# TensorE's instructions in the order in which the source writes them, in a hybrid attention layer

## The chip, the core and the metric

The kernel runs on one core of one Trainium2 chip. The metric is device time in microseconds (us) of one execution of the whole layer; lower is better.

## The reference

One decoder layer over 2048 positions of width 1024, in float32. A normalised input is projected by one matrix into queries, keys, values and gates of two mixers. Mixer A attends over a window of 128 positions with a learned sink per head; mixer B attends under three dilated patterns and merges them by their softmax denominators. Both results are gated, joined, projected out and added to the input.

```python
hdn = rmsnorm(x, norm_gain[i])
proj = jnp.einsum("bsd,de->bse", hdn, w_in[i])
q_a, k_a, v_a, g_a, q_b, k_b, v_b, g_b = jnp.split(proj, split_at, axis=-1)
...
o_a, _, _ = banded_attention(q_a, k_a, v_a, A_WINDOW - 1, sinks=sinks_a[i])
o_a = o_a.reshape(b, S, A_WIDTH).astype(x.dtype) * jax.nn.silu(g_a)
...
o_b = dilated_attention(q_b, k_b, v_b)
o_b = o_b.reshape(b, S, B_WIDTH).astype(x.dtype) * jax.nn.silu(g_b)

mixed = jnp.concatenate([o_a, o_b], axis=-1)
x = x + jnp.einsum("bse,ed->bsd", mixed, w_out[i])
```

## The kernel before

**Stages.** The work is cut into eight stages (line 26): four of mixer B with two heads each, two of mixer A with four query heads each, and two halves of the output projection. A stage goes over four blocks of 512 positions, a block over two halves of 256. Each half multiplies its inputs by the stage's weights: for every 128 positions (`tt`) 24 matmuls into a PSUM tile `pj` (line 244), then the gates, 24 matmuls for each 128 gate columns into another `pj`. Every product is made of three matmuls, since operands are split into a high and a low part (`wh`, `wl`, `xh`, `xl`) for precision.

**Behind a projection** stand three chains. `norm_rope`, `norm_factors` and `norm_split` (lines 406 to 461) normalise and rotate queries and keys on VectorE, ScalarE and GpSimd; `finish` and `qk_transposes` (lines 342 and 463) then transpose them on TensorE and copy the result out of PSUM. For the first stage, `rstd` (line 193) sums squares of x with four small matmuls, takes the root on GpSimd, and `rb_make` (line 208) transposes the result on TensorE.

**Attention units.** One head of one block is a unit of four steps: `scores` (matmuls into `sc`, then a masked maximum on VectorE, lines 598 and 813, and an exponential on ScalarE, lines 599 and 814), `transposes` (TensorE turns the probabilities `P` into `pt`; `split_p`, lines 573 and 574, copies them out as a high part on ScalarE and a low part on VectorE), `pv` (matmuls with the values into `po`), and `after`. A unit over the window (lines 590 to 645, and 719 to 735 in mixer A) works in four blocks of 128 queries. A dilated unit (lines 808 to 849) makes a triangle of scores in three `sc` tiles, whose first holds two of the four query blocks, and three `pt` tiles.

**Buffers.** PSUM holds two tiles of each of the names `pj`, `sc`, `pt` and `po`: a third tile of a name begins when the first has been read out.

**The order.** The source itself interleaves: `proj` is a generator that yields after every few matmuls, and `advance` (line 931) then issues one step of a unit, so that the steps keep pace with the projection by their estimated costs. The program is then handed to the scheduler of the tile framework, which takes the source's order as priorities and issues on each engine what its timing simulation finds ready. So a step that waits lets later instructions of the same engine pass. All DMAs are issued by SyncE (SP).

The steps of the prediction touch these lines: 198 (`rstd`), 211 (`rb_make`), 244 (projection), 475, 485, 490, 491 and 499 (`qk_transposes`), 590 and 591 (window scores), 619, 625 and 719 (their transposes), 645 and 735 (their products), 808 and 809 (dilated scores), 828 and 835 (their transposes), 849 (their product).

Of the kernel before, what the change touches and what calls it, by code (L numbers as in the profile page):

```python
# [32 lines left out]
@with_exitstack  # L33
def hybrid_layer(ctx, tc, xT, xn, x, wB, wA, wO, ng, gains, sinks, rot, masks, ident, out):
    nc = tc.nc
    PS = bass.MemoryType.PSUM
    const = ctx.enter_context(tc.tile_pool(name="const", bufs=1))
    wp = ctx.enter_context(tc.tile_pool(name="wp", bufs=1))
# [2 lines left out]
    wk = ctx.enter_context(tc.tile_pool(name="wk", bufs=2))  # L41
    ps = ctx.enter_context(tc.tile_pool(name="ps", bufs=1, space=PS))

# [996 lines left out]
```

## Time and profile before

| | us |
|---|---|
| median of 3 runs | 1261.07 (1257.18 to 1261.21) |
| profiled execution, its own time | 1261.51 |
| profiled execution, span of its instructions | 1259.4 |

The page is one execution on the chip. Busy time of an engine is the union of its instructions. Matmuls overlap: one lasts longer from its start to its end than the time until the next may start, so TensorE (PE) counts as busy through short waits. PEld are its weight loads, which run ahead of the matmuls. DVE is VectorE, ACT ScalarE, POOL GpSimd. "L244" is line 244 of the kernel. A row of waits names who waited, for whose result, how long in total, how often, and the longest. PEclk is the share of its full clock that TensorE was granted.

### The profile page before, as it was taken

The page shows a single profiled execution, that of the slowest core. Times are in us where ns is not written, and L with a number is a line of the kernel's source. Part 1 is how long each engine was busy: PE and PEld are TensorE (multiplying, and loading weights), DVE is VectorE, ACT ScalarE, POOL GpSimd, SP SyncE. Part 2 cuts the span into 40 slices and gives each one's busy share as a digit, 9 for nine tenths or more (in the row PEclk, how much of TensorE's full clock was granted, in tenths as well). Part 3 has the DMA queues.
Part 4 walks back from the last instruction along what each step waited for, and adds up shares of the span by engine and source line. Part 5 has one row for each costly group of instructions (what it writes and reads, how often), then busy time and mean ns, then how long its engine had stood idle before and what let it go on. Part 6 is the DMA issues. An engine that isn't in the chain of part 4 may idle for free.

```text
span 1259.4 us, 25438 instructions
## 1 busy us (share of the span) xinstructions
PE 1174.8 (93%) x8328; PEld 1141.3 (91%) x8328; DVE 850.7 (68%) x2288; ACT 834.7 (66%) x2418; POOL 680.4 (54%) x788
## 2 busy tenths in 40 slices
PE   6898979899899798899998999999999999999899
PEld 5898979899799798888997999898899998999898
DVE  5676768678677678776777788789868877522221
ACT  6477868678677687676777677677776776522221
POOL 4886734566645574536576567565655554333122
PEclk9899989999899899899998999999999999999999
DMA  7454677877687667687775764545333225566561
GB/s 215 120 166 127 193 226 212 229 200 212 182 250 207 210 190 201 189 244 204 199 210 172 228 203 143 150 137 167 114 97 94 80 89 165 163 192 211 166 191 69
DMA packets 196883, 220.98 MB, mean 175 GB/s; under 512 B 34312, under 2 KB 143632, under 8 KB 196752
## 3 DMA queue, kind: packets, MB, share of 16 engines
q1 hardware_dynamic: 196752, 219.37, 59.3%
q8 instruction: 66, 1.08, 0.4%
q14 instruction: 65, 0.53, 0.1%
HBM read 164.44 MB, written 54.86 MB: 174 GB/s over the span
## 4 chain that ended last, share of the span: by engine, by line
PE 55%; DMA 16%; DVE 10%; ACT 8%; POOL 6%; issue 3%; SPq 2%; POOLq 0%; ACTq 0%; DVEq 0%
PE pj L244 39%; DMA xs<-in_xT 3%; DMA Rb<-rD 2%; DMA stg<-in_wB 2%; PE po L849 2%; DMA stg<-in_wO 2%; DMA stg<-in_wA 2%; PE sc L590 1%; PE sc L591 1%; PE po L645 1%; PE pt L828 1%; PE po L735 1%; PE pt L719 1%; ACT P L599 1%; DVE ptl L574 1%
## 5 line engine op out<-in xcount | busy, mean ns | idle before, releaser
L244 PE MATMUL pj<-wh,xh 128*128 128x384 f32 (+1 forms) x1008 | 332.8, 332 | 12.2 <-ACT wh L104 5.5
L244 PE MATMUL pj<-wl,xh 128*128 128x384 f32 (+1 forms) x1008 | 334.4, 332 | 0.8 <-DVE wl L102 0.7
L244 PE MATMUL pj<-wh,xl 128*128 128x384 f32 (+1 forms) x1008 | 333.4, 331 | 1.3 <-DVE xl L157 1.3
L157 POOL TENSOR_TENSOR xl<-xs,xh 128x512 fp32r<-128x512 f32 x158 | 210.3, 1341 | 146.3 <-ACT xh L155 136.6
L155 ACT ACTIVATE xh<-xs 128x512 fp32r<-128x512 f32 x252 | 154.5, 629 | 123.6 <-PE pj L244 100.6
L244 PEld LDWEIGHTS pj<-wh,xh 128*128 128x128 f32 x1008 | 194.0, 193 | 15.7 <-ACT wh L104 5.8
L244 PEld LDWEIGHTS pj<-wl,xh 128*128 128x128 f32 x1008 | 194.8, 193 | 3.2 <-DVE wl L102 1.1
L244 PEld LDWEIGHTS pj<-wh,xl 128*128 128x128 f32 x1008 | 194.4, 193 | 3.0 <-DVE xl L157 1.6
L574 DVE TENSOR_TENSOR ptl<-pt,pth 128x512 fp32r<-128x512 f32 (+3 forms) x232 | 142.0, 619 | 35.5 <-ACT pth L573 31.8
L244 PE MATMUL pj<-xh,wgh 128*128 128x256 f32 x496 | 147.7, 298 | 17.9 <-DVE V L311 12.0
L244 PE MATMUL pj<-xh,wgl 128*128 128x256 f32 x496 | 145.8, 294 | 0.0
L244 PE MATMUL pj<-xl,wgh 128*128 128x256 f32 x496 | 145.4, 293 | 0.0
L573 ACT ACTIVATE pth<-pt 128x512 fp32r<-128x512 f32 (+3 forms) x232 | 123.1, 543 | 23.1 <-PE pt L719 8.1
L431 POOL TENSOR_TENSOR t<-t,t 128x256 f32<-128x256 f32 (+1 forms) x96 | 78.1, 814 | 77.9 <-DVE t L422 57.2
L244 PEld LDWEIGHTS pj<-xh,wgh 128*128 128x128 f32 x496 | 97.8, 197 | 19.7 <-ACT klz L502 5.9
L244 PEld LDWEIGHTS pj<-xl,wgh 128*128 128x128 f32 x496 | 97.8, 197 | 0.6
L244 PEld LDWEIGHTS pj<-xh,wgl 128*128 128x128 f32 x496 | 97.4, 196 | 0.9 <-DVE wgl L105 0.2
L814 ACT ACTIVATE P<-P,scD 128x256 f32<-128x256 f32 (+3 forms) x128 | 71.6, 560 | 33.6 <-DVE scD L813 32.9
L157 DVE TENSOR_TENSOR xl<-xs,xh 128x512 fp32r<-128x512 f32 x94 | 76.9, 823 | 21.1 <-ACT xh L155 20.5
L447 DVE TENSOR_TENSOR t<-t,fac 128x256 f32<-128x256 f32 (+1 forms) x96 | 67.4, 710 | 30.8 <-POOL fac L182 23.7
L182 POOL TENSOR_TENSOR fac<-un,mhalf 128x8 f32<-128x8 f32 (+1 forms) x48 | 85.4, 1779 | 2.5
L813 DVE CUSTOM_DVE_ANT_0 P<-sc,mk 128x256 f32<-128x256 f32 (+3 forms) x128 | 61.1, 484 | 32.2 <-PE sc L809 31.5
(188 smaller groups left out, 3082.8 us busy)
## 6 DMA issues: line engine op xcount, KB each, us to landing
xs<-in_xT SPq DMA_DIRECT2D x94, 512.0 KB
xs<-mx SPq DMA_DIRECT2D x32, 512.0 KB
vd<-V SPq DMA_DIRECT2D x64, 128.0 KB
qd<-qc SPq DMA_DIRECT2D x32, 256.0 KB
TT<-tab SPq DMA_DIRECT2D x32, 256.0 KB
cv<-vd SPq DMA_DIRECT2D x32, 256.0 KB
cq<-qd SPq DMA_DIRECT2D x32, 256.0 KB
ck<-kd SPq DMA_DIRECT2D x64, 128.0 KB
```

What stands on the lines that cost most here:

```text
L155: nc.scalar.activation(h, f, AF.Copy)
L157: eng.tensor_tensor(l, f, f32(h), op=OP.subtract)
L182: nc.gpsimd.tensor_tensor(y, u, mhalf.to_broadcast([128, n]), op=OP.pow)
L244: nc.tensor.matmul(o, a, b, start=first and n == 0, stop=last and n == 2, skip_group_check=True)
L431: nc.gpsimd.tensor_tensor(t1[:, :n], t1[:, :n], t2[:, :n], op=OP.add)
L447: nc.vector.tensor_tensor(t1v, t1v, fac[:, tt, :, None].to_broadcast([128, nh, 64]), op=OP.mult)
L573: nc.scalar.activation(hi, pt, AF.Copy)
L574: nc.vector.tensor_tensor(lo, pt, f32(hi), op=OP.subtract)
L590: nc.tensor.matmul(sc[:, j, :], q[h // 2][:, h % 2, i, :], kw, start=True, stop=False)
L813: nc.vector.tensor_tensor_reduce(pd, o[:, :m], m2[:, 512 - m:], -0.125, BIG, OP.add, OP.min, nb)
L814: nc.scalar.activation(pd, pd, AF.Exp, bias=nb, scale=-1.0, accum_out=l)
L849: nc.tensor.matmul(po[:, o:o + w], a, b, start=n_ == 0, stop=n_ == len(seq) - 1, skip_group_check=True)
```

## The change

One line is added at the head of `hybrid_layer`:

```diff
     nc = tc.nc
+    ctx.enter_context(tc.manual_schedule(engines={mybir.EngineType.PE}))
     PS = bass.MemoryType.PSUM
```

Inside this context TensorE's instructions stay in the order in which the source issues them. The scheduler still orders the other four engines and SyncE's DMAs, now around that fixed order. The instructions are the same: 8296 matmul instructions before and after, and the same number of operations on every other engine. All source lines move down by one, so line 828 before is line 829 after, and the numbers in tile names grow by two.

**Dilated unit.** TensorE, fourth stage, last block, the unit whose probabilities are `P_10230` before and `P_10232` after; `pt` tiles are its three transposed tiles, `pj` is the projection beside it, `po` the product of another unit. Before:

```order
L828 MATMUL pt_10360<-idf_75,P_10230 128x128
L244 MATMUL pj_10334<-wh_9499,xh_10284 128x384
L828 MATMUL pt_10360<-idf_75,P_10230 128x128 x2
L244 MATMUL pj_10334<-wl_9500,xh_10284 128x384
L849 MATMUL po_10338<-ptl_88,cv_9884 128x256 x2
L828 MATMUL pt_10367<-idf_75,P_10230 128x128 x2
L244 MATMUL pj_10334<-wh_9499,xl_10285 128x384
```

After, the same unit:

```order
L245 MATMUL pj_10336<-wh_9488,xl_10151 128x384
L829 MATMUL pt_10362<-idf_77,P_10232 128x128 x4
L829 MATMUL pt_10369<-idf_77,P_10232 128x128 x3
L836 MATMUL pt_10375<-idf_77,P_10232 128x128 x3
L245 MATMUL pj_10336<-wh_9501,xh_10286 128x384
```

Before, the transposes are strewn among the projection's matmuls, and the third tile (line 835) comes 28 rows after the last transpose into the second; after, all ten stand in one piece.

**Window unit of mixer A.** TensorE, the unit with probabilities `P_14224` before and `P_14226` after; `sc` tiles take its scores, `pt_14188` and `po_14250` belong to other units. Before:

```order
L719 MATMUL pt_14188<-idf_75,P_13894 128x128 x4
L590 MATMUL sc_14225<-KK_13431,Q_13429 128x256
L591 MATMUL sc_14225<-klz1_90,Q_13429 128x256
L590 MATMUL sc_14225<-KK_13431,Q_13429 128x256
L591 MATMUL sc_14225<-klz1_90,Q_13429 128x256
L244 MATMUL pj_14176<-xh_13835,wgh_12729 128x256
```

After:

```order
L591 MATMUL sc_14227<-KK_13433,Q_13431 128x256
L592 MATMUL sc_14227<-klz1_92,Q_13431 128x256
L591 MATMUL sc_14227<-KK_13433,Q_13431 128x256
L592 MATMUL sc_14227<-klz1_92,Q_13431 128x256
L591 MATMUL sc_14236<-KK_13433,Q_13431 128x256
L592 MATMUL sc_14236<-klz1_92,Q_13431 128x256
L591 MATMUL sc_14236<-KK_13433,Q_13431 128x256
L592 MATMUL sc_14236<-klz1_92,Q_13431 128x256
L672 MATMUL po_14250<-idf_77,eA_14245 8x128
L720 MATMUL pt_14256<-idf_77,P_14226 128x128 x4
L720 MATMUL pt_14263<-idf_77,P_14226 128x128 x4
```

Before, 37 more rows stand between these four score matmuls and the unit's first transposes, and the last two of its eight score matmuls come only behind those; after, one row stands between all eight and the transposes.

**The start.** TensorE, first half; `po` holds the transposed root of `rb_make`, `sc` the projection of the second half. Before:

```order
L244 MATMUL pt_404<-xh_171,wgl_249 128x256
L211 MATMUL po_305<-idf_75,rst_83 128x128 x2
L198 MATMUL po_381<-one_81,o1c_321 128x1 x4
L244 MATMUL sc_462<-wh_135,xl_365 128x384
L244 MATMUL sc_462<-wh_144,xh_364 128x384
```

After:

```order
L199 MATMUL po_207<-one_83,o1c_195 128x1 x4
L245 MATMUL pj_263<-wh_117,xh_112 128x384
L245 MATMUL pj_263<-wl_118,xh_112 128x384
L245 MATMUL pj_263<-wh_117,xl_113 128x384
L245 MATMUL pj_263<-wh_126,xh_112 128x384
```

These five rows open TensorE's program after: the sums of squares come ahead of the first projection, and `rb_make` (line 212) follows right behind that projection's 24 matmuls. Before, 97 rows of matmuls stand ahead of `rb_make`. SP and POOL begin with the same operations in the same order in both programs, through GpSimd's first root (line 182).

## The prediction

> **What bounds the kernel now.** I read the page's engine rows first, then the waits of TensorE, then its timeline at the steps that the change moves.
>
> ```profile
> span 1259.4 us, 25438 instructions
> PE 1174.8 (93%) x8328; PEld 1141.3 (91%) x8328; DVE 850.7 (68%) x2288; ACT 834.7 (66%) x2418; POOL 680.4 (54%) x788
> ```
>
> TensorE is the bound: 1174.8 of 1259.4 us, next VectorE with 68%. So 84.6 us of it are idle, and no order of the same instructions can win more than these and what a low clock costs. The waits show who ends the idle time:
>
> ```profile
> PE pj L244 <- DVE V L311: 13.2, 7, 5.7
> PE sc L591 <- ACT klz L502: 5.8, 2, 4.7
> PE pj L244 <- ACT wh L104: 5.5, 1, 5.5
> PE pt L828 <- DVE ptl L574: 5.2, 2, 5.0
> PE po L499 <- ACT KK L478: 4.8, 1, 4.8
> PE po L211 <- POOL rst L182: 4.3, 1, 4.3
> ```
>
> They are few and long: the largest sum, 13.2 us, comes from seven waits. At none of the attention steps is there a wait each time. The groups by shape say the same of the step that interests us most, the third transposed tile of a dilated unit:
>
> ```profile
> L835 PE MATMUL pt<-idf,P 128*128 128x128 f32 x96 | 15.9, 273 | 0.7 <-DVE ptl L574 0.7
> L499 PE MATMUL po<-idr,hl 128*128 128x128 f32 x64 | 10.8, 251 | 5.3 <-ACT KK L478 4.8 <-DVE osum L570 0.5
> ```
>
> 96 transposes by three a unit are 32 units, with 0.7 us of idle time ahead of them altogether. They don't wait, because projection matmuls stand in between. The change takes exactly these away.
>
> **The clock.** Idle time costs twice here. The core's row gives the mean granted clock, the windows show one short and one long idle stretch, each with the stretch behind it:
>
> ```profile
> core 0: 1259.4 us, clock 0.969
> 605.00:606.80 1.80, 0.08 (x1) 0.08 (x1) 1.80 (x4) 0.10 (x1) 1.80 (x2) 1.00 0.89 238
> 606.90:610.30 3.40, 3.40 (x12) 3.40 (x13) 3.28 (x11) 3.35 (x13) 1.54 (x4) 0.50 0.99 276
> 27.30:31.60 4.30, 0.02 (x1) 0.02 (x1) 0.00 (x0) 1.50 (x3) 4.22 (x4) 0.82 0.67 210
> 31.60:36.80 5.20, 5.20 (x20) 5.20 (x21) 5.00 (x6) 1.47 (x5) 5.20 (x7) 0.50 0.01 1
> ```
>
> 1.8 us without work are followed by 3.4 us at half clock, which lose 1.7 us; 3.1% of 1259.4 us is 39 us lost to the clock in all.
>
> **The change, part by part.** It removes and adds no operation. In place of "what is ready" TensorE now takes "what comes next", so each wait of a step holds the whole engine. I go through the steps whose next neighbour in the source is the one that needs their result.
>
> *Third tile of a dilated unit (line 835).* Two `pt` tiles exist, so it waits until ScalarE and VectorE have read the first. Shortest case of the 32, from the timeline:
>
> ```profile
> 721.29 0.34 PE L244 MATMUL pj<-wl,xh 128*128 128x384 f32 x1
> 721.47 0.38 PE L828 MATMUL pt<-idf,P 128*128 128x128 f32 x2
> 721.77 0.98 ACT L573 ACTIVATE pth<-pt 128x512 fp32r<-128x512 f32 x2 [1.33 <-PE pt L828]
> 722.41 0.69 DVE L574 TENSOR_TENSOR ptl<-pt,pth 128x512 fp32r<-128x512 f32 x1 [1.23 <-ACT pth L573]
> ```
>
> From the last transpose into the first tile (721.47) to the end of VectorE's pass (723.10) it takes 1.63 us. In the new order that transpose itself and the three into the second tile fill 0.11 us each, 0.44 us. So 1.2 us of stall, times 32: 38 us with free engines. The longest of this kind in the waits is 5.0 us. VectorE is busy two thirds of the time, so I take 1.6 us, near the free case: **51 us**.
>
> *Scores of a dilated unit (line 808).* The second query block shares a tile with the first and waits until VectorE has read that; the fourth needs the same tile again.
>
> ```profile
> 189.50 0.29 PE L809 MATMUL sc<-cl,cq 128*128 128x256 f32 x1
> 189.83 0.29 DVE L813 CUSTOM_DVE_ANT_0 P<-sc,mk 128x128 f32<-128x128 f32 x1 [2.36 <-PE sc L809]
> 192.79 0.42 DVE L813 CUSTOM_DVE_ANT_0 P<-sc,mk 128x256 f32<-128x256 f32 x1
> ```
>
> The matmul at 189.50 is out of the way 0.12 us later, VectorE ends at 190.12: 0.5 us. For the fourth block 0.33 us to VectorE's start and 0.42 us of its pass stand against 0.12 us of the matmul and 0.36 us of the third block's two: 0.3 us. Together 0.8 us, times 32: 26 us; with a queue on VectorE up to twice that. I take 1.1 us: **35 us**.
>
> *Third `po` tile of `qk_transposes`.*
>
> ```profile
> L477 ACT ACTIVATE Q<-po 128x256 fp32r<-128x256 f32 x64 | 24.2, 377 | 8.0 <-PE po L475 8.0
> L478 ACT ACTIVATE KK<-po 128x256 fp32r<-128x256 f32 x64 | 24.6, 384 | 0.0
> ```
>
> Two copies of 0.38 us behind a handover of 0.3 us (721.47 to 721.77 above) are 1.06 us, less some 0.4 us of transposes into the second tile: 0.65 us in each of 32 halves of mixer B, 21 us. Mixer A has four tiles in a half, and two of them wait, by the same rows some 1.2 us in 16 halves: 19 us. With a little queueing: **45 us**, bounds 25 and 100 (4.8 us is the longest such wait above, in one place).
>
> *Scores, transposes, product of a lone unit.* Where only one unit is in flight, the source puts its transposes right behind its scores. One such passage, late in mixer A:
>
> ```profile
> 1080.01 0.28 PE L591 MATMUL sc<-klz,qc 128*128 128x256 f32 x1
> 1083.01 0.19 ACT L599 ACTIVATION_READ_ACCUMULATOR P<-P,scA 128x1 f32 x1
> ```
>
> 3.2 us from the last score's start to the last exponential's end. In the new order 15 units (eight of mixer B, seven of mixer A) have between 0.7 and 1.9 us of TensorE's work there, counted in matmuls of 0.12 and 0.18 us: some 2 us of stall each, 30 us. Their product follows in the same way behind two passes of ScalarE and VectorE, some 25 us more. **55 us**, bounds 25 (free engines) and 110.
>
> *The start and `rb_make`.* TensorE's third place is `rb_make`, which needs the root from GpSimd, and GpSimd's order up to there is unchanged:
>
> ```profile
> 22.89 7.95 POOL L90 TENSOR_SCALAR klz<-mk 64x640 fp32r<-64x640 f32 x4
> 30.81 0.72 POOL L182 TENSOR_TENSOR rst<-rss,mhalf 128x2 f32<-128x2 f32 x1
> 0.00:31.50 31.50, 19.63 (x103) 17.59 (x103) 18.20 (x40) 20.05 (x44) 14.73 (x20) 0.98 0.72 215
> 47.24 0.52 PE L244 MATMUL pj<-wh,xh 128*128 128x384 f32 x1
> ```
>
> By 31.5 us TensorE had issued 103 matmuls before; after, 28. The rest of the first two halves is 72 matmuls of 0.18 us (721.11 to 721.29 is such a step) and 48 of 0.12 us, 18.8 us, and some 2 us more at half clock: the third half begins at about 52 in place of 47.24 us. That is 5 us. `rb_make` returns seven times in the first stage, right behind the gates; 2 us each, from 0 to the 4.3 us of the wait above. Together **20 us**, bounds 3 and 36.
>
> *Normalised queries and keys (line 475 on POOL's `hl`).* Some 11.5 us of projection stand between the last matmul of a half and its transposes, and attention steps besides. No row prices the chain behind; the nearest is a single wait of 2.6 us.
>
> ```profile
> PE po L475 <- POOL hl L458: 2.6, 1, 2.6
> L182 POOL TENSOR_TENSOR fac<-un,mhalf 128x8 f32<-128x8 f32 (+1 forms) x48 | 85.4, 1779 | 2.5
> ```
>
> Between nothing and 2.6 us in each of 48 halves (GpSimd's root, 1.8 us, is taken once a half), I take **10 us**.
>
> The sum is 51 + 35 + 45 + 55 + 20 + 10 = 216 us. These stalls don't simply add: while TensorE stands, ScalarE and VectorE work off what the next step waits for. I count two thirds, 144 us; that share is a choice, with one half and the whole as its ends (108 and 216).
>
> *What goes.* Of the 84.6 us, 5.5 at the start stay in any order. Waits on `V`, `klz` and `KK` arise where the scheduler let projections or units run ahead of their buffers; I take 50 of the 79 us as gone. *Clock:* the 15 lone units and the start give new idle stretches of 2 us and more, a few go; +15 us net. Short stalls of 0.5 to 1.6 us I leave without this cost.
>
> 1261.5 us (the profiled execution's own time; the median, 1261.1, is the same within 0.1%) + 144 - 50 + 15 = **1370 us**.
>
> **The rivals.**
>
> *The clock drops at every dilated unit.* Its scores and its transposes stall within a few microseconds of each other, and the rows at 605 show 1.8 us to be enough. 32 units twice and 15 lone ones, 79 stretches at 1.7 us, are 134 us in place of today's 39: 1261.5 + 144 - 50 + 95 = **1450 us**. Against it: a dilated unit's stalls are shorter than that one and apart.
>
> The Trainium skill, page "TensorE: Matmul & The Clock Gate", section "A second HAM failure mode: psum-queue depth-cycling", says that small idle gaps between groups of matmuls can make the clock swing between half and full; by it this rival would be the likelier one. The same page's section "Part 1: The HAM clock gate" puts half clock behind an idle window of about 3.4 us, by which nearly none of the new stalls would cost it; the 1.8 us above disagree with that.
>
> *The norm chain becomes late in every half.* 2.6 us in 48 halves are 125 us, two thirds 83, in place of 7: **1446 us**. For it: the root alone takes 1.8 us, and three engines take turns in the chain. Against it: 11.5 us of cover.
>
> *The order settles everything, and it gets faster.* If the waits on run-ahead (`V`, `klz`, `KK`, weights) all go with their low clock, 79 + 30 us, and only the stalls in the dilated units remain at their lowest, 38 + 26 us, the time is 1261.5 - 109 + 64 = **1217 us**. It decides where all new stalls together stay under 109 us. Against it: my bounds with free engines already come to 38 + 26 + 25 + 25 + 3 = 117 us. *The same:* new stalls just fill the old idle time, **1261 us**.
>
> **How the numbers follow.** Forecast (1310 to 1420) 0.62; clock rival 0.15; norm chain 0.11; slower, but under 1310, 0.04; same 0.03; faster 0.05. A measurement of this kernel can tell about 0.3% from no change. The range leaves out the faster and equal cases and the far end of the two slow rivals: 1295 to 1470.
>
> **What would show it.** Line 836 should have some 50 us of idle time ended by VectorE's `ptl` (line 575), in 32 waits; line 809 some 35 us by line 814; 500, 486 and 491 some 45 us by ScalarE's copies; 620, 626 and 720 waits on the exponential of line 600; the first `rb_make` should stand at about 31.5 us. The waits on `V` should shrink. Many stretches of clock 0.5 in the dilated units would speak for the first rival, waits of `hl` in every half for the second. I am wrong if line 836 hardly waits, or if TensorE's idle time stays near 85 us.

## The result and the profile after

The changed kernel takes **1481.43 us** (median of 4 runs, 1474.12 to 1485.73) against 1261.14 us beside it: ratio **1.174** (95% interval 1.167 to 1.181), 220 us more. The forecast was 1370 us with a range up to 1470: the direction holds, the size is half of what came.

| profiled execution | before | after |
|---|---|---|
| its own time, us | 1261.5 | 1478.4 |
| span, us | 1259.4 | 1476.6 |
| granted clock | 0.969 | 0.946 |
| time lost to the clock (span by one less the clock), us | 39 | 80 |

The page's span and engine rows of after, and its core's row:

```profile
span 1476.6 us, 25365 instructions
PE 1256.8 (85%) x8328; PEld 1175.1 (80%) x8328; DVE 854.8 (58%) x2288; ACT 853.5 (58%) x2418; POOL 672.6 (46%) x788
core 0: 1476.6 us, clock 0.946
```

The work of VectorE, ScalarE and GpSimd is the same within 20 us. TensorE's idle time rises from 84.6 to 219.8 us, by 135 us, and its busy time by 82 us though it runs the same matmuls. So the idle column alone shows only some 60% of the 217 us.

TensorE's waits after, the largest in order and then those that the prediction named:

```profile
PE pt L836 <- DVE ptl L575: 48.8, 31, 2.4
PE sc L809 <- DVE scD L814: 28.0, 57, 1.7
PE po L500 <- ACT KK L479: 26.3, 29, 4.5
PE po L199 <- DVE o1c L192: 18.8, 4, 14.0
PE po L486 <- ACT qc L488: 15.4, 8, 5.4
PE pt L720 <- ACT P L600: 11.4, 25, 1.4
PE pt L620 <- ACT P L600: 7.4, 11, 2.3
PE po L212 <- POOL rst L183: 7.2, 2, 5.6
```

Before, waits were few and long; now line 836 waits 31 times, line 809 57 times, line 500 29 times. The one large wait of before, of `pj` on `V` (13.2 us), is no longer among them. The groups by shape show the same at the two third tiles, whose counterparts of before had 0.7 and 5.3 us:

```profile
L836 PE MATMUL pt<-idf,P 128*128 128x128 f32 x96 | 19.0, 311 | 50.9 <-DVE ptl L575 48.8 <-DMA ck<-kd 2.1
L500 PE MATMUL po<-idr,hl 128*128 128x128 f32 x64 | 11.8, 267 | 26.3 <-ACT KK L479 26.3
```

**Where the 217 us are.** Since a stalled matmul's predecessor still counts as busy until its end, I worked from starts. The page counts 8328 matmuls in each kernel (the 8296 in the section on the change are 32 too few). For each I took the time from its start to the next one's start, less the usual spacing of its shape at full clock (0.174 us for 384 columns, 0.119 for 256, 0.232 for 512, 0.11 for a transpose of probabilities, 0.06 to 0.08 for one of queries and keys). What is left is a stall, put down to the matmul that came late; the part of it that a half clock explains is counted apart. The spacings add to some 1115 us in both kernels.

| us, by the matmul that came late | before | after | difference | prediction |
|---|---|---|---|---|
| third tile of a dilated unit (836) | 1 | 58 | +57 | 51 |
| scores of a dilated unit (809, 810) | 6 | 46 | +40 | 35 |
| `qk_transposes` (476 to 500) | 8 | 69 | +60 | 45, and 10 for `hl` |
| lone units: transposes (620, 626, 720) and products (646, 736) | 15 | 62 | +47 | 55 |
| start: first matmul (at 5.5 and 14.0 us), `rstd`, `rb_make` | 13 | 27 | +14 | 20 |
| sum of the new stalls | | | **+217** | **216**, then two thirds: **144** |
| projections, window scores, first tiles (829) | 72 | 35 | -37 | -50 |
| half clock while matmuls run | 26 | 60 | +35 | +15 |

The sums are made from tenths. With 2 us at small steps they make the 217 us of the two spans' difference. So every place but the norm chain's (`hl`) was right, and every price within a third of its size; that the two sums differ by 1 us only is in part luck, as errors of -10 to +15 us cancel. What failed is what was done with the sum.

### The profile page after: what moved, and what is told of

It is laid out like the page before. It is cut to its first block, busy times and chain, and to the rows that moved or that the text cites. A ratio compares the mean times of both kernels' runs of the same rounds, so it can differ in the third digit from the quotient of the medians.

```text
span 1476.6 us, 25365 instructions
## 1 busy us (share of the span) xinstructions
PE 1256.8 (85%) x8328; PEld 1175.1 (80%) x8328; DVE 854.8 (58%) x2288; ACT 853.5 (58%) x2418; POOL 672.6 (46%) x788
## 5 line engine op out<-in xcount | busy, mean ns | idle before, releaser
L245 PE MATMUL pj<-wh,xh 128*128 128x384 f32 (+1 forms) x1008 | 336.5, 334 | 1.8 <-ACT wh L102 1.3
L245 PE MATMUL pj<-wl,xh 128*128 128x384 f32 (+1 forms) x1008 | 330.7, 328 | 3.1 <-DVE wl L106 3.0
L575 DVE TENSOR_TENSOR ptl<-pt,pth 128x512 fp32r<-128x512 f32 (+3 forms) x232 | 139.0, 620 | 75.3 <-ACT pth L574 74.6
L245 PE MATMUL pj<-xh,wgh 128*128 128x256 f32 x496 | 151.3, 305 | 0.0
L574 ACT ACTIVATE pth<-pt 128x512 fp32r<-128x512 f32 (+3 forms) x232 | 117.8, 541 | 44.2 <-PE pt L836 22.3
L815 ACT ACTIVATE P<-P,scD 128x128 f32<-128x128 f32 (+3 forms) x128 | 71.5, 559 | 50.1 <-DVE scD L814 49.7
L414 DVE TENSOR_REDUCE un<-sq 128x4 f32<-128x256 f32 (+1 forms) x96 | 42.2, 440 | 98.5 <-ACT sq L411 98.1
L411 ACT ACTIVATE sq<-pj 128x256 f32<-128x256 f32 (+1 forms) x94 | 37.3, 396 | 100.5 <-PE pj L245 99.7
L183 POOL TENSOR_TENSOR fac<-un,mhalf 128x8 f32<-128x8 f32 (+1 forms) x48 | 84.6, 1763 | 1.6
```

The source lines that it names most:

```text
L183: nc.gpsimd.tensor_tensor(y, u, mhalf.to_broadcast([128, n]), op=OP.pow)
L245: nc.tensor.matmul(o, a, b, start=first and n == 0, stop=last and n == 2, skip_group_check=True)
L411: nc.scalar.activation(sq[:, :n], pj[:, :n], AF.Square, scale=0.125)
L414: nc.vector.tensor_reduce(uv, sq[:, :n].rearrange("p (h d) -> p h d", d=64), axis=AX.X, op=OP.add)
L574: nc.scalar.activation(hi, pt, AF.Copy)
L575: nc.vector.tensor_tensor(lo, pt, f32(hi), op=OP.subtract)
```

## The experiments

All kernels below start from the changed kernel, with TensorE in source order, unless the text says otherwise. Their ratios are to the kernel before, which ran on the same chip beside them. Three of the edits lend a tile a buffer of another name, which removes a wait that the prediction named.

**e1_pt: the third tile of a dilated unit takes a `po` buffer.**

```diff
                 s["sp"] = sp
-                pt = ps.tile([128, 4, 128], F32, name="pt", bufs=2)
+                pt = ps.tile([128, 4, 128], F32, name="po", bufs=2)
```

> TensorE's order fixed as in the change, but the third transposed tile of each dilated unit takes a po buffer, so that it need not wait until the first has been read out. Theory A (the new stalls add one to one, and the low clock comes on top): the wait at line 836 goes, 51 us of idle time and about 6 us of pipeline ends, and with it some 20 us of half clock; about 1404 us (1390 to 1425). Theory B (stalls overlap, as the prediction's two thirds had it: the engines that are late at one step are early at the next, so a removed wait comes back elsewhere): at most 38 us less, 1440 us or more.

Measured: 1440.48 us, ratio 1.146 (1.142 to 1.149), 41 us below the changed kernel, or 36 by ratios. The waits of this kernel that had been smaller, and the third tile's group:

```profile
PE sc L809 <- DVE scD L814: 40.2, 62, 2.3
PE po L646 <- DVE ptl L575: 19.7, 8, 5.9
L836 PE MATMUL po<-idf,P 128*128 128x128 f32 x96 | 16.0, 276 | 0.0
```

The stall is gone (0.0 us), but by starts of matmuls 14 us come back at the dilated scores and 11 us at the window products. That is at B's bound of 1440; A's 1404 isn't reached. More is saved than nothing, less than the whole stall.

**e2_po: the last tiles of `qk_transposes` take `sc` buffers**, in mixer B the third tile, in mixer A both tiles of the second 128 positions. The edit of mixer B:

```diff
-            pt = ps.tile([128, 2, 128], F32R, name="po", bufs=2)
+            pt = ps.tile([128, 2, 128], F32R, name="sc", bufs=2)
             for tt, hl in enumerate(hls):
```

> TensorE's order fixed; the last tiles of the query and key transposes take sc buffers in place of a third po tile. Theory A: the waits of lines 500, 486 and 491 on ScalarE's copies go (44 us of idle time, about 55 with pipeline ends) and some 15 us of half clock; about 1410 us (1395 to 1430). Theory B: at most 37 us less, 1444 us or more.

Measured: 1451.54 us, ratio 1.156 (1.151 to 1.160), 30 us less, or 23 by ratios. The stalls there fell from 69 to 6 us; some 33 us came back at the projections, window products and window scores, as B had it (1444 or more); A's 1410 isn't reached.

**e12_both: both edits.**

> Both edits together. Theory A: the gain is the sum of the two single gains within 15 us; about 1335 us. Theory B: with both ways of slowing closed, the gain is larger than the sum of the single gains by 25 us or more.

Measured: 1418.43 us, ratio 1.129 (1.125 to 1.133), 63 us below the changed kernel; by ratios 57 us, where the two alone make 36 and 23. The savings add, as A had it in kind, since the second edit finds as much to save beside the first as alone; A's 1335 us, which took each saving for a whole stall, is far off.

**e3_sc: all score matmuls of a dilated unit ahead of its maxima, the fourth block in a `pt` buffer.**

```diff
+                os = []
                 for t in range(4):
...
-                        sc = ps.tile([128, 512], F32, name="sc", bufs=2)
+                        sc = ps.tile([128, 512], F32, name="pt" if t == 3 else "sc", bufs=2)
...
+                    os.append(o)
...
+                for t in range(4):
+                    o = os[t]
```

> TensorE's order fixed; a dilated unit's first two score blocks are multiplied ahead of both their max passes, and the fourth block takes a pt buffer. Theory A: the waits of line 809 on VectorE go (28 us of idle time, 37 with pipeline ends), little clock; a few us come back where the pt buffer is still being read; about 1443 us (1430 to 1460). Theory B: under 25 us, 1456 us or more.

Measured: 1439.55 us, ratio 1.144 (1.139 to 1.150), 42 us less. Of this step's 46 us 1.5 are left; 10 come back at the transposes that follow (line 833). Their waits are for the exponential (7.2 us on line 819) and not, as A expected, for the lent `pt` buffer. A's 1443 is met.

**e5_fill: work in the gap.** Ten transposes that nobody reads go into the free fourth column of the second `pt` tile of each dilated unit, 320 in all, ahead of the stalled step.

```diff
                         nc.tensor.transpose(pt[:, t - kt, :], blk(t, kt), idf)
+                    for _ in range(10 if kt else 0):
+                        nc.tensor.transpose(pt[:, 3, :], blk(3, 1), idf)
```

> As the change, with ten more transposes in every dilated unit, into a column of its second transposed tile that nobody reads: 320 in all, 1.1 us a unit, put where TensorE stands before the third tile. They compute nothing that is used. The wait itself stays, but TensorE is active in it. Theory C (the half clock behind these stalls is a cost of its own; 11 of the 37 half-clock stretches after the change begin within 3.6 us of a wait at line 836): half-clock time falls by some 40 us and the time by 12 to 22 us, to about 1463 us. Theory D (the clock follows other stalls, or what it costs is hidden by the next wait): half-clock time and time stay within 6 us, or the time rises by the delay of the second tile, up to 10 us.

Measured: 1458.39 us, ratio 1.160 (1.156 to 1.164): with 320 more matmuls the kernel is 23 us **faster** (17 us by ratios). Its rows:

```profile
PE 1275.1 (88%) x8648; PEld 1194.1 (82%) x8648; DVE 854.5 (59%) x2288; ACT 854.0 (59%) x2418; POOL 671.4 (46%) x788
core 0: 1455.7 us, clock 0.962
PE pt L838 <- DVE ptl L575: 14.5, 19, 1.1
```

Line 838 is the third tile here. The new transposes take 34 us and its stall shrinks by 35 us, so they cost nothing; what is won is the clock, 0.946 to 0.962, 19 us less lost while matmuls run. Theory C, some 1463 us, is met: a part of the price of the stalls is the clock.

**e4_burst: at most one attention step after each piece of projection**, in place of as many as are due.

```diff
-            while (pending or pipe) and done < total * pr / pcost[kind]:
+            if (pending or pipe) and done < total * pr / pcost[kind]:
...
-                    break
+                    continue
```

> TensorE's order fixed; between two yields of the projection the source issues at most one attention step in place of as many as the pace asks for, so bursts of steps of one unit are drawn apart: 16 units in place of 31 have under 2 us of TensorE's work between any scores and their transposes. Theory A: of the waits on exponentials and split probabilities (lines 620, 626, 720, 646 and 736; 35 us of idle time, some 50 with pipeline ends) half goes, with some clock; about 1450 us (1430 to 1465). Rival: steps held back pile up at the end of a block and in the output projection, and the waits only move; within 10 us of 1481 us or above.

Measured: 1493.06 us, ratio 1.187 (1.183 to 1.191), slower by 12 us, as the rival had it. By starts the waits that the edit aimed at stay at some 60 us together, and the third tile, whose wait lies inside one step, goes from 58 to 68 us:

```profile
PE pt L836 <- DVE ptl L575: 61.4, 32, 4.2
PE pt L720 <- ACT P L600: 15.6, 32, 1.6
```

**e123 and e1234_all: the first three edits together, and with e4_burst's.**

> The three edits of e1_pt, e2_po and e3_sc together, each stall of the dilated units and of the queries' and keys' transposes given another buffer or place. By ratio to before, the changed kernel was 1.174, and the three took 0.028, 0.018 and 0.030 off it alone. A (each stall is paid in full and by itself): the three add, ratio 1.097, some 1383 us, range 1372 to 1392. B (stalls overlap, one removed returns at the next step; the prediction's two thirds): they take off no more than two thirds of their sum, ratio 1.123 or above, 1415 us or more.

> TensorE's order fixed, with all four source edits (third transposed tile in a po buffer, last key and query tiles in sc buffers, score blocks of the dilated unit regrouped, at most one step between yields). Adding: the three single gains measured so far (36, 23 and 37 us, scaled to the same kernel before) and 25 us for the fourth, 121 us in all: about 1360 us (1340 to 1380). If waits come back elsewhere as more ways are closed: 1390 us or more.

Measured: e123 1392.81 us, ratio 1.105 (1.098 to 1.113), e1234_all 1377.05 us, ratio 1.096 (1.092 to 1.101). Nine tenths of the sum of the three single savings arrive together in e123 (0.069 of 0.076), just past the end of A's range and far from B's; e1234_all lies inside the adding theory's range, near its end. So savings add. That a stall is paid in full is not shown by it: by starts the three edits, one by one, take away 165 us of stall (58, 63 and 44), and together they save 87 us by ratios. The two intervals overlap, so what the fourth edit does here isn't settled. The waits of the lone units, which no edit lends a buffer, remain, and the order still costs about a tenth. The largest waits of e1234_all:

```profile
PE po L199 <- DVE o1c L192: 19.7, 3, 14.2
PE po L646 <- DVE ptl L575: 19.4, 6, 6.2
PE pt L720 <- ACT P L600: 14.5, 34, 1.2
PE pt L833 <- ACT P L819: 14.5, 12, 1.4
```

**s1234_sched: the same four edits with the scheduler's order.**

> The same four source edits without the change: TensorE back with the scheduler. Theory: the scheduler fills these waits with projection matmuls already, so the edits are worth little there: 1245 to 1270 us, within 1% of before. Rival: the buffers themselves were short in both orders, and it gains 2% or more.

Measured: 1263.35 us, ratio 1.005 (1.002 to 1.008). What takes some 7% off in source order is worth nothing here, as the theory had it: the scheduler had already filled these waits with projection.

**e1236: e123 with a start in another order.** The sums of squares go behind the first projection tile, `rb_make` behind the first gate matmuls (the second move is shown).

```diff
             fac = norm_factors(nh, sb, half, un)
-            RB = RBS.pop((si, hf))
...
+                if gc == 0:
+                    if si == 0:
+                        rb_make(hf)
+                    RB = RBS.pop((si, hf))
```

> As e123, and beside it the sums of squares of the first half moved behind its first projection tile, and rb_make moved in front of the use of its result, behind the gate matmuls. A (the start and rb_make cost what the starts of the matmuls show, some 14 us, and the low clock with it): 12 to 20 us below e123, first matmul at about 5.5 us again. B (the start is bound by the loads of x and the weights and by GpSimd's root, whatever stands first): within 5 us of e123.

Measured: 1392.97 us, ratio 1.107 (1.101 to 1.113), the same as e123. The first matmul starts at 5.9 in place of 14.9 us, and the 120th of the order 12.9 us earlier; by the 180th only 3.6 us are left. The timeline of e1236 shows what took them:

```profile
42.65 0.83 PE L199 MATMUL po<-one,o1c 128*128 128x1 f32 x6 [1.73 <-DVE o1c L192]
47.41 0.75 PE L477 MATMUL po<-idr,hl 128*128 128x128 f32 x4 [3.92 <-POOL hl L460]
49.84 0.75 PE L477 MATMUL po<-idr,hl 128*128 128x128 f32 x4 [1.69 <-POOL hl L460]
```

The first normalised queries and keys leave GpSimd at 47.8 us here and at 49.8 us in e123. So the start is bound by that chain, and a TensorE that arrives 12.9 us earlier mostly waits there. The norm chain of the prediction's second rival exists, but once, at the start.

**p_dil: scheduler, with the order kept only among a dilated unit's own transposes.**

```diff
+                with tc.manual_schedule(engines={mybir.EngineType.PE}):
+                    transposes_()
+
+            def transposes_():
```

> The scheduler orders TensorE again, and only the transposes of a dilated unit among themselves keep the source's order; the projection may come in between. A (what costs is that nothing else may pass a waiting step, not the order inside the step): within 0.7% of before, 1252 to 1270 us, and the third pt tile waits less than 5 us in all. B (the order inside the step is itself what makes the third tile late): idle time of 30 us or more ahead of the third tile, 1290 us or more.

Measured: 1271.61 us, ratio 1.011 (1.007 to 1.016); the third tile's group:

```profile
L839 PE MATMUL pt<-idf,P 128*128 128x128 f32 x96 | 15.7, 273 | 0.4 <-DVE ptl L574 0.4
```

The order inside the step costs the third tile nothing as long as projection may pass. The time is 1.1% above before, a little outside A's 0.7%; by starts the largest parts are window scores, `qk_transposes` and dilated products, 8 to 9 us each, and why is not settled.

**o1_col3 and o2_col3: a stall removed without a lent buffer.** Is the price of a stall only a share of its length, or did the lent buffers of e1_pt take something back? Both kernels leave out the third group of probabilities. (The 41 us that "came back" in the first expectation are the 41 us that e1_pt saved.)

```diff
-                pt = ps.tile([128, 4, 128], F32, name="pt", bufs=2)
-                for b, (t, kt) in enumerate(((2, 2), (3, 2), (3, 3))):
-                    nc.tensor.transpose(pt[:, b, :], blk(t, kt), idf)
+                for t, kt in ((2, 2), (3, 2), (3, 3)):
+                    nc.tensor.transpose(pt[:, 3, :], blk(t, kt), idf)
```

> The third transposed tile of each dilated unit is left out: its three transposes stay, but go into the free fourth column of the second tile, and ScalarE and VectorE read the second tile a second time in its place; the third group of probabilities is wrong. So TensorE, ScalarE and VectorE do the same operations, line 835 has no buffer to wait for, and no other name lends one, as it did in e1_pt, where the stall of 57 us went and 41 us came back. A (what a stall costs is what the starts of the matmuls show, and in e1_pt the rest returned because a po tile was lent): 50 to 65 us below the changed kernel, ratio 1.122 to 1.134, 1412 to 1427 us. B (stalls overlap whatever buffer is used, two thirds of a stall is what it costs): about as e1_pt, ratio 1.138 to 1.150, 1432 to 1447 us, with more waits at the dilated scores and at the products.

Measured: 1498.94 us, ratio 1.196 (1.192 to 1.200), outside both:

```profile
PE pt L835 <- DVE ptl L575: 69.4, 32, 3.5
```

The transposes into the free column now wait for VectorE's pass over the *second* tile, though they touch other columns than it reads. The Trainium skill, page "PSUM — Partial Sum Buffer", section "PSUM bank collisions raise a hardware error ⚠️", has a rule that asks for such a wait: two engines may not touch one bank's partitions at the same time, at other addresses either, and PSUM has to be guarded by bank. The 32 waits agree with it, but no run here tells whether that rule or the framework's book-keeping by whole tiles put them in. The edit missed its aim and became the opposite test: 19 us more of stall by starts (77 in place of 58) made the kernel 18 us longer in its own median and 28 us by ratios. In o2_col3 the three stand ahead of the passes, so nothing is left to wait for:

> As o1_col3, but the three transposes into the fourth column of the second tile stand ahead of ScalarE's and VectorE's passes over that tile, so that nothing is left for them to wait for: the order of TensorE is that of the changed kernel row by row. The third group of probabilities is left out, its passes read the second tile again. A (a stall is paid in full; what returned in e1_pt came from the lent po tile): 50 to 65 us below the changed kernel, ratio 1.122 to 1.134, 1412 to 1427 us. B (two thirds of a stall is what it costs, the rest returns at the next steps though no buffer is lent): ratio 1.138 to 1.150, 1432 to 1447 us, the scores of the dilated units or the products waiting some 15 us more than in the changed kernel.

Measured: 1449.19 us, ratio 1.155 (1.152 to 1.157), 32 us less than the changed kernel, or 24 by ratios. Its rows:

```profile
L832 PE MATMUL pt<-idf,P 128*128 128x128 f32 x96 | 16.0, 276 | 0.0
PE sc L809 <- DVE scD L814: 38.8, 61, 2.4
PE po L646 <- ACT pth L574: 23.8, 7, 7.5
```

58 us of stall are gone and no buffer is lent; by starts 12 us come back at the dilated scores, 18 at the window products, 10 at the dilated products, while some 14 us less go to the clock. The time lies outside both ranges. B is right in kind, a stall shelters others, and more came back than B says: only 41 to 55% of the 58 us are saved.

## Why the prediction was right in direction and wrong in size

**Places and prices: right.** Line 836 was to have some 50 us by line 575 in 32 waits: 48.8 us in 31. Line 809 some 35: 28.0 us idle, 40 by starts. Lines 500, 486 and 491 some 45 by ScalarE's copies: 44 us idle (26.3 and 15.4 above and 2.6 for 491), 60 by starts. (Another 7.3 us ahead of line 486 stand under POOL's `un`; in the timeline these waits end right behind ScalarE's second copy, 858.98 and 859.07 us in one of them, so they are of the same kind.) Lines 620, 626 and 720 wait on line 600 as said. The first `rb_make` was to stand at about 31.5 us and stands at 30.41. The waits on `V` are gone.

**The failed step: "These stalls don't simply add ... I count two thirds, 144 us."** In place they add to 217 us, and 73 of the missing 108 us are this step. The reason given was that ScalarE and VectorE work off what the next step waits for while TensorE stands. That happens when a stall is removed: by starts, 26 of 58 us come back at other steps in e1_pt and 41 of 58 in o2_col3. But in the changed kernel no discount showed at any of the three steps that I had priced with free engines: the third tile stands at 57 us against 38, the dilated scores at 40 against 26, the `qk_transposes` at 60 against 40 (21 and 19). In a fixed order the passes that TensorE waits for also queue behind others on their engines. The timeline of after at a dilated unit, with those rows of TensorE, ScalarE and VectorE that bear on its first tile:

```profile
646.69 0.36 PE L500 MATMUL po<-idr,hl 128*128 128x128 f32 x2 [0.71 <-ACT KK L479]
647.09 0.78 ACT L503 ACTIVATE klz<-po 64x256 fp32r<-64x256 f32 x2
647.32 0.93 PE L829 MATMUL pt<-idf,P 128*128 128x128 f32 x7
647.90 0.51 ACT L350 ACTIVATE KK<-KK 128x128 fp32r<-128x128 f32 x2
648.31 0.62 ACT L353 ACTIVATE klz<-klz 64x128 fp32r<-64x128 f32 x2
648.96 0.98 ACT L574 ACTIVATE pth<-pt 128x512 fp32r<-128x512 f32 x2
649.59 0.69 DVE L575 TENSOR_TENSOR ptl<-pt,pth 128x512 fp32r<-128x512 f32 x1 [2.39 <-ACT pth L574]
650.34 0.66 PE L836 MATMUL pt<-idf,P 128*128 128x128 f32 x3 [2.10 <-DVE ptl L575]
```

ScalarE is still copying the queries and keys of the step before (lines 503, 350, 353) and reaches the first tile 1.6 us after its first transpose. From the last transpose into the first tile to the third tile I had 1.63 us from the shortest case; over the 32 units it is 1.68 to 2.98 us, 2.19 in the mean and over 2.4 in fourteen. In twelve of the fourteen ScalarE begins its pass 1.07 to 1.32 us after that last transpose, against 0.31 in the shortest units: in nine it runs lines 503, 350 and 353 first, as here, in three lines 457 and 458. In the other two VectorE runs line 448 ahead of its pass. So the queue adds 0.56 us a unit, 18 us in all, to the 38 us with free engines, which makes up the 57. My 51 us held 13 us for queueing already, and the discount came on top of a price that needed none. This is worked out for the third tile only; that the queue outweighs the relief in the same way at the other steps is argued from their sums, and how much relief the measured stalls contain is not shown.

**The clock term: 15 us, measured 35** (by the mean clock 39 to 80 us, 41 more). I left "short stalls of 0.5 to 1.6 us ... without this cost". The windows of after, over that same unit and the stretch behind it:

```profile
646.70:650.60 3.90, 1.80 (x14) 1.57 (x15) 1.51 (x4) 3.14 (x10) 3.59 (x5) 1.00 0.59 160
650.60:654.00 3.40, 2.35 (x10) 1.66 (x9) 2.86 (x9) 2.10 (x8) 2.48 (x5) 0.51 0.68 154
654.00:657.50 3.50, 3.50 (x12) 3.11 (x13) 2.28 (x12) 2.10 (x8) 0.00 (x0) 0.51 0.91 255
```

In 3.9 us TensorE is busy for 1.8, the 2.1 us wait being one piece; 6.8 us at half clock follow (the third column from the right is the granted clock). The trace of after has 37 such stretches, 17 before, and in 12 of them a wait of line 836 lies within the 3.6 us ahead. The stretches of both traces begin on a raster of 3.41 us and last one, two or three of its windows. Sorted by TensorE's idle time, the windows of both traces at full clock show what counts: of 459 with under 1.2 us one was followed by half clock, of 45 with 1.2 to 1.75 us twelve, of 40 with more 39. So it is the idle time within one window, in one piece or in several. Here three waits of 0.43, 0.36 and 0.54 us (lines 620 and 626) make 1.39 us in the first window:

```profile
104.50:107.90 3.40, 2.01 (x13) 1.15 (x12) 1.60 (x6) 3.40 (x15) 3.40 (x8) 1.00 0.88 218
107.90:111.30 3.40, 3.40 (x16) 3.34 (x16) 2.03 (x9) 2.63 (x9) 0.88 (x3) 0.50 0.54 131
```

That is what my term left out: the short stalls of one window add up. The first rival named the right mechanism, but with 79 stretches where there are 37 and +95 us where 35 were measured. Its 1450 us are nearer to the result than my forecast only because this excess offsets part of the two thirds that it shares; e5_fill shows the clock's share. The Trainium skill, page "TensorE: Matmul & The Clock Gate", section "Part 1: The HAM clock gate", asks for an idle window of about 3.4 us; here 1.75 us within a window of 3.41 us were enough in 39 of 40 cases. The Trainium skill, page "TensorE: Matmul & The Clock Gate", section "A second HAM failure mode: psum-queue depth-cycling", by which small gaps between groups of matmuls make the clock swing, agrees in kind with the window at 104.5 us.

**What goes: 50 us, measured 37.** The waits of window scores and first tiles went nearly all, those of the projections from 53 to 34 us.

**The parts put right**: 1261.5 + 217 - 37 + 35 = 1476.5, and 2 us at small steps, against 1478.4.

**The other rivals.** The norm chain didn't become late in every half: line 476 has no wait on POOL's `hl` in the trace of after, and the 10 us I put there didn't come; it shows only in e1236, in the first half. Faster and equal fell: the new stalls are six times what the order saved, and even with three sources of them gone (e123) the order costs a tenth.

**What stays open.** Where e123 stands 131 us above before is known by starts: 46 us at the window products, 24 at the transposes of window units, 18 by the clock, 16 at the start, and 6 to 11 at each of four other steps; the projections' 54 us are those of before. e4_burst left these waits of the lone units as they were, and no run removes them. Open are also how much relief the measured stalls contain, and the 1.1% of p_dil.

## What to carry to other kernels

When an engine's order is fixed, price each step whose next neighbour needs its result by the whole stall, with the queue on the engines that it waits for, and add the prices up. Take no discount for overlap from that sum: here the three steps priced with free engines came out above those prices. Expect a removed stall to give back only a part of its length: four to nine tenths here, the clock included, and about half for three together. A two-buffer name with a third tile in one step, cheap under a scheduler, cost some 1.8 us each time in source order here; what helps is other work that may pass, which buffers lent from elsewhere replaced only in part. Read the cost of short stalls from starts and from the granted clock, since the busy column hides what an idle engine loses.

## What was not expected of the hardware

More work made the kernel faster: 320 useless transposes in a stall took 19 us off the time that the low clock costs (granted clock 0.946 to 0.962). TensorE need not stand still for a whole window to lose the clock: with over 1.75 us of idle time in one of 3.41 us, 39 of 40 windows were followed by half clock. A window at half clock must itself be busy to end it: all 13 with 1.0 us or more of idle time were followed by another, and 4 of 46 with less. So a single wait of 2.1 us cost 6.8 us at half clock, as TensorE was idle for another 1.05 us in the first half of them. And of the 217 us more, 82 stand in TensorE's busy column: some 35 are the lower clock, and the rest I put down to the ends of the last matmuls ahead of each wait, which count as busy: TensorE has 249 gaps of over 0.05 us in place of 59.
